# A SwiGLU feed-forward with its down products laid between the block products, on a ring of ten hidden tiles

## Chip, core and metric

The kernel runs on one core of one Trainium2 chip. The metric is the device time of one launch in microseconds (us).

## What is computed

One step of a layer over 520 columns, 512 of a prompt and 8 samples. All of it is in float32.

```python
def half_ffn(x, g, w1, w3, w2):
    h = rmsnorm(x, g)
    return x + 0.5 * ((jax.nn.silu(h @ w1) * (h @ w3)) @ w2)
...
x = half_ffn(x, ...)          # first feed-forward
x = x + mixer(rmsnorm(x))     # short convolution and dilated attention
x = half_ffn(x, ...)          # second feed-forward
y = rmsnorm(x)
```

The width is 1024 (8 blocks of 128) and the hidden width 2816 (22 blocks). The change is in the two feed-forwards.

## The kernel before

**Layout.** The residual lies in SBUF transposed, as eight tiles X[0..7] of 128 features by 520 columns, and every product is done in two halves of 260 columns. A float32 operand is split into a high and a low part of a type that TensorE takes, and `mm3` makes a product from three matmuls: high x high, high x low, low x high. `load_w` brings a block of weights (`raw`, four buffers), ScalarE writes its high part and VectorE its low part (three buffers each).

**A feed-forward (`ffn`)** has four sorts of work.
- Its norm: `rstd_rows` sums squares over the partitions with matmuls (L178, L179) and gives `rbc`, one over the root mean square of each column. The operand of part 0 is X times the gain, split (L135, L136), without the norm; the norm is put on the products after. In the first feed-forward the first three block products are laid ahead of this (`early`), step by step as X arrives.
- Part 0: the hidden blocks 0 to 3, each a plain product of w1 and one of w3 (48 matmuls each), then silu, a multiplication, and the split into `hh` and `hl`. After each block `x_sums(k)` prepares seven sums and differences of normed X blocks, tiles `sh` and `sl` in the pool `xo`.
- The blocks 4 to 21 in nine pairs (`pair(m)`): a pair's two blocks of w1 come out of seven quarter-size products (`seven`, 7 x 12 matmuls) in the way of Strassen and Winograd, and its two blocks of w3 out of another seven. `seven` needs sums of weights (`ws`, L363 to L366, on VectorE), their splits (L372 on ScalarE, L373 on VectorE), and copies and additions of what the products leave in PSUM (L380 to L392). The last additions (L386, L390, L392) stand on VectorE.
- `down(w2, k0, k1)`: the hidden blocks k0 to k1 times w2, added to X. It is eight products, one for each X tile, of 6 matmuls for each hidden block, and each ends in an X update by VectorE (L404), one instruction for each half.

**Order.** `CUTS = (0, 4, 14, 22)`: part 0, then `down` over it; pairs 4 to 12, `down` over these ten blocks; pairs 14 to 20, `down` over the last eight, which in the second feed-forward is interlocked with the final norm (`finish`, `give`). The order within an engine is set before the run by the tile framework, which plans the program in time with the order of the code as priority. Within each engine instructions then run in that order.

**PSUM.** `psum_tile` hands out tiles of two banks: two buffers of the tag "mm" and one of "m3", in the order mm, mm, m3. Tiles of one tag are given out in order.

**SBUF.** Pools stack up from the left and from the right, and a pool may lie on bytes that a closed pool held; its tiles then wait for that one's users. In the feed-forward `gu` (12,480 bytes a partition), `hida` (four hidden blocks, 16,640) and `hidb` (six more, 24,960) lie left from byte 84,640 on; `xo` (58,368), then `xa` (33,280, the operand of part 0) or, later, `su` (the weight sums) lie right. After the first feed-forward the mixer takes `yp` and `ap` left and `xam` right (33,280 bytes, up to byte 229,344), its operand.

Of the kernel before, what the change touches and what calls it, by code (L numbers as in the profile page):

```python
# [13 lines left out]
P = 128  # L14
# [24 lines left out]
CUTS = (0, 4, 14, 22)  # L39
# [12 lines left out]
def tile_step(ctx: ExitStack, tc: tile.TileContext, xT, w0, w1a, w3a, w2a, w_in, w_out, w1b, w3b, w2b,  # L52
# [173 lines left out]
    def ffn(i, w1, w3, w2, g, psum, finish=None):  # L226
        turn = [0]
# [15 lines left out]
        with ExitStack() as st:  # L243
            gu = st.enter_context(tc.tile_pool(name=f"gu{i}", bufs=1, reuse_waits="tile"))
            hids = [st.enter_context(tc.tile_pool(name=f"hida{i}", bufs=1, reuse_waits="tile"))]
            with ExitStack() as sx:
                xo = sx.enter_context(tc.tile_pool(name=f"xo{i}", bufs=1, side="right", reuse_waits="tile"))
                with tc.tile_pool(name=f"xa{i}", bufs=1, side="right", reuse_waits="tile") as xa:
                    early = []

                    def start_x():
                        SP.dma_start(gv, gvec)
                        SP.dma_start(X[0][:, TH:], xT[:, 0, TH:])

                    if i == 0:
                        SP.dma_start(X[0][:, :TH], xT[:, 0, :TH])
                        for k in range(0, KD, 2):
                            if k:
                                SP.dma_start(X[k], xT[:, k])
                            early.append(load_w(w0[k // 2], 6, [slice(0, 3), slice(3, 6)] if not k else None, then=start_x if not k else None))  # L260
                            SP.dma_start(X[k + 1], xT[:, k + 1])
                        SP.dma_start(ident, idm)
                    xh, xl, sums = x_operand(xa, f"f{i}", g, i == 0)

                    def norm_tiles():
                        t = psum_tile()
                        return [t[:, h] for h in range(2)]

                    rstd_rows(norm_tiles, sums, D, rbc)
                    if early:  # L270

                        early, ws = [psum_tile() for _ in range(3)], early
                        for k in range(KD):
                            for e, ps in enumerate(early):
                                hi, lo = (t[:, 3 * (k % 2) + e] for t in ws[k // 2])
                                for h in range(2):
                                    c = slice(h * TH, (h + 1) * TH)
                                    mm3(ps[:, h, :TH], hi, lo, xh[k][:, c], xl[k][:, c], k == 0, k == KD - 1)
                    xs = []
                    for m in range(CUTS[1]):  # L280
                        pp = []
                        a = gu.tile([P, T], F32, name="a", tag="a", bufs=2)
                        b = gu.tile([P, T], F32, name="b", tag="b")
                        for w, t in ((w1, a), (w3, b)):
                            if early:

                                A.activation(halves(t), early.pop(0)[:, :, :TH], AF.Copy)
                                pp.append(halves(t))
                                continue
                            hi, lo = load_w(w[m], KD)  # L290
                            ps = psum_tile()
                            gemm(ps, [(hi, lo, 0, KD)], xh, xl)
                            pp.append(ps[:, :, :TH])
                        V.tensor_tensor(halves(a), pp[0], halves(rbc), ALU.mult)
                        A.activation(a, a, AF.Silu)
                        V.tensor_tensor(halves(b), pp[1], halves(rbc), ALU.mult)
                        V.tensor_tensor(b, b, a, ALU.mult)
                        hh, hl = hidden(m)
                        A.activation(hh, b, AF.Copy)
                        V.tensor_tensor(hl, b, hh.bitcast(F32), ALU.subtract)  # L300

                        xs.append(x_sums(xo, xa, f"f{i}", g, m))
                    down(w2, 0, CUTS[1], Hh, Hl, psum_tile)
                hids.append(st.enter_context(tc.tile_pool(name=f"hidb{i}", bufs=1, reuse_waits="tile")))
                su = sx.enter_context(tc.tile_pool(name=f"su{i}", bufs=2, side="right", reuse_waits="tile"))

                def pair(m):

                    at, aw, bt = psum_tile(), psum_tile(), psum_tile()
                    a = gu.tile([P, 4, TH], F32, name="a", tag="a", bufs=2)  # L310
                    b = gu.tile([P, 4, TH], F32, name="b", tag="b")
                    x = seven(su, w1, m, xs, at, aw[:, 0, :TH], a)
                    A.activation(a[:, 0:2], a[:, 0:2], AF.Silu)
                    A.activation(a[:, 3], a[:, 3], AF.Silu, scale=-1.0)
                    A.activation(a[:, 2], x, AF.Silu, scale=-1.0)
                    x = seven(su, w3, m, xs, bt, aw[:, 1, :TH], b)
                    V.tensor_tensor(b[:, 0:2], b[:, 0:2], a[:, 0:2], ALU.mult)
                    V.tensor_tensor(b[:, 3], b[:, 3], a[:, 3], ALU.mult)
                    V.tensor_tensor(b[:, 2], x, a[:, 2], ALU.mult)
                    for r, sign in ((0, 1.0), (1, -1.0)):  # L320
                        hh, hl = (halves(t) for t in hidden(m + r))
                        of = b[:, 2 * r:2 * r + 2]
                        A.activation(hh, of, AF.Copy, scale=sign)
                        if r:
                            V.scalar_tensor_tensor(hl, of, sign, hh.bitcast(F32), ALU.mult, ALU.subtract)
                        else:
                            V.tensor_tensor(hl, of, hh.bitcast(F32), ALU.subtract)
# [67 lines left out]
    def down(w2, k0, k1, Hh, Hl, psum_tile, finish=None):  # L395
# [18 lines left out]
        if not finish:  # L414
            return
# [522 lines left out]
```

## Time and profile before

| | |
|---|---|
| time, median of 3 runs | 1033.15 us (1032.54 to 1035.03) |
| the profiled execution: its time | 1036.0 us |
| its span (first to last instruction) | 1034.2 us |
| mean granted clock of TensorE | 0.981 |
| busy: TensorE matmul (PE) | 996.0 us, 96% |
| TensorE weight load (PEld, overlaps PE) | 965.4 us, 93% |
| VectorE (DVE) | 726.5 us, 70% |
| ScalarE (ACT) | 505.0 us, 49% |
| GpSimd (POOL) | 92.2 us, 9% |

Busy time is that of the profiled execution. Consecutive matmuls overlap in the records, so a stretch of TensorE can count as busy though matmuls follow each other more slowly than they could. A row of the trace names an engine, the line of the kernel, the operation, and the tiles written and read.

### The profile page before, as it was taken

What the parts mean: (1) busy time and instruction counts of PE and PEld (TensorE: products, weight loads), DVE (VectorE), ACT (ScalarE), POOL (GpSimd) and SP (SyncE); (2) the same over time, 40 slices, a digit from 0 to 9 for tenths busy, and PEclk for the clock granted to TensorE, in tenths of its full rate; (3) what the DMA queues carried; (4) which work ended last, traced back from release to release, by engine and by line L of the source; (5) the groups of instructions that cost most, each with busy time, mean ns of one, the idle gap of its engine ahead of it and who ended that gap; (6) DMA issues with size and microseconds to landing.
All of it is one profiled execution on the core that took longest, in us unless ns stands there. A gap on an engine that the chain in (4) does not pass through costs nothing.

```text
span 1034.2 us, 19174 instructions
## 1 busy us (share of the span) xinstructions
PE 996.0 (96%) x7897; PEld 965.4 (93%) x7897; DVE 726.5 (70%) x1193; ACT 505.0 (49%) x833; POOL 92.2 (9%) x103
## 2 busy tenths in 40 slices
PE   6999999999999999999999998999999999999997
PEld 5999999999999999999999897999998999999897
DVE  6788888436786546667688799797887634788332
ACT  4534565323555436566565545443555422555342
POOL 1000000000000031112022263000000000000022
PEclk6999999999999999999999999999999999999998
DMA  6325434354443445243246665325334233333302
GB/s 208 113 90 186 144 131 140 105 183 156 148 157 125 143 141 173 83 144 129 66 146 222 205 203 184 103 82 184 133 125 151 64 90 113 102 103 103 101 22 83
DMA packets 37912, 136.62 MB, mean 132 GB/s; under 512 B 5760, under 2 KB 8512, under 8 KB 37312
## 3 DMA queue, kind: packets, MB, share of 16 engines
q1 hardware_dynamic: 37824, 135.39, 39.2%
q8 instruction: 62, 1.02, 0.4%
q14 instruction: 26, 0.21, 0.1%
HBM read 131.07 MB, written 37.82 MB: 163 GB/s over the span
## 4 chain that ended last, share of the span: by engine, by line
PE 70%; DVE 15%; DMA 6%; issue 4%; ACT 4%; POOL 1%; SPq 0%; POOLq 0%; DVEq 0%; ACTq 0%
PE ps L121 22%; PE ps L123 21%; PE ps L122 21%; DVE lo L373 3%; DMA raw<-in_w1b 2%; DVE lo L109 2%; DMA raw<-in_w3b 2%; DVE ls L373 1%; ACT hi L108 1%; PE s L568 1%; DMA raw<-in_w1a 1%; DVE ws L364 1%; DVE raw L365 1%; ACT hi L372 1%; DVE ws L363 1%
## 5 line engine op out<-in xcount | busy, mean ns | idle before, releaser
L108 ACT ACTIVATE hi<-raw 128x1024 fp32r<-128x1024 f32 (+3 forms) x136 | 119.1, 878 | 215.6 <-PE ps L122 167.3
L121 PE MATMUL ps<-hh,hi 128*128 128x260 f32 x704 | 200.5, 287 | 4.3 <-ACT hi L108 3.5
L123 PE MATMUL ps<-hh,lo 128*128 128x260 f32 x704 | 200.8, 286 | 1.5 <-DVE lo L109 1.4
L122 PE MATMUL ps<-hl,hi 128*128 128x260 f32 x704 | 199.9, 285 | 0.5 <-DVE hl L300 0.3
L109 DVE TENSOR_TENSOR lo<-raw,hi 128x1024 fp32r<-128x1024 f32 (+3 forms) x136 | 143.6, 1057 | 74.9 <-ACT hi L108 74.0
L121 PEld LDWEIGHTS ps<-hh,hi 128*128 128x128 f32 x704 | 133.5, 191 | 6.8 <-ACT hi L108 4.3
L123 PEld LDWEIGHTS ps<-hh,lo 128*128 128x128 f32 x704 | 134.0, 190 | 3.0 <-DVE lo L109 2.5
L122 PEld LDWEIGHTS ps<-hl,hi 128*128 128x128 f32 x704 | 134.0, 190 | 1.2 <-DVE hl L300 1.2
L121 PE MATMUL ps<-mh,hi 128*128 128x260 f32 x384 | 110.3, 288 | 1.8 <-DVE q L498 1.1
L123 PE MATMUL ps<-mh,lo 128*128 128x260 f32 x384 | 109.3, 285 | 0.3 <-DVE u L619 0.3
L122 PE MATMUL ps<-ml,hi 128*128 128x260 f32 x384 | 109.4, 285 | 0.0
L372 ACT ACTIVATE hi<-raw 128x1024 fp32r<-128x1024 f32 x72 | 75.7, 1053 | 60.8 <-PE ps L122 58.2
L144 POOL TENSOR_TENSOR acc<-acc,sq 128x520 f32<-128x520 f32 (+1 forms) x25 | 38.3, 1530 | 752.9 <-ACT sq L143 748.8
L373 DVE TENSOR_TENSOR lo<-raw,hi 128x1024 fp32r<-128x1024 f32 x72 | 87.5, 1217 | 4.8 <-ACT hi L372 4.8
L372 ACT ACTIVATE hs<-ws 128x1024 fp32r<-128x1024 f32 x72 | 60.5, 840 | 54.0 <-DVE ws L364 48.0
L121 PE MATMUL ps<-f1sh,hi 128*128 128x260 f32 x288 | 82.1, 285 | 3.4 <-DVE X L404 1.2
L121 PE MATMUL ps<-f0sh,hi 128*128 128x260 f32 x288 | 82.2, 286 | 2.0 <-ACT a L384 1.7
L122 PE MATMUL ps<-f0sl,hi 128*128 128x260 f32 x288 | 81.4, 283 | 0.0
L123 PE MATMUL ps<-f1sh,lo 128*128 128x260 f32 x288 | 80.2, 282 | 1.3 <-DVE lo L373 1.2
L122 PE MATMUL ps<-f1sl,hi 128*128 128x260 f32 x288 | 81.3, 283 | 0.0
L123 PE MATMUL ps<-f0sh,lo 128*128 128x260 f32 x288 | 79.6, 282 | 0.0
L404 DVE SCALAR_TENSOR_TENSOR X<-ps,X 128x260 f32<-128x260 f32 x96 | 36.7, 422 | 57.9 <-PE ps L123 57.9
(278 smaller groups left out, 2744.8 us busy)
## 6 DMA issues: line engine op xcount, KB each, us to landing
out_cko<-in_ck SPq DMA_DIRECT2D x16, 1023.0 KB, 7.1
out_cvo<-in_cv SPq DMA_DIRECT2D x16, 1023.0 KB, 7.2
raw<-in_w_in SPq DMA_DIRECT2D x24, 512.0 KB, 3.3
raw<-in_w1b SPq DMA_DIRECT2D x22, 512.0 KB, 3.3
raw<-in_w3b SPq DMA_DIRECT2D x22, 512.0 KB, 3.3
raw<-in_w3a SPq DMA_DIRECT2D x21, 512.0 KB, 3.3
raw<-in_w1a SPq DMA_DIRECT2D x20, 512.0 KB, 3.3
raw<-in_w2a SPq DMA_DIRECT2D x16, 320.0 KB, 3.0
```

The lines of the kernel that those rows point to most:

```text
L108: A.activation(hi, raw, AF.Copy)
L109: V.tensor_tensor(lo, raw, hi.bitcast(F32), ALU.subtract)
L121: PE.matmul(out, lhsT=hi, rhs=xh, start=start, stop=False, skip_group_check=more)
L122: PE.matmul(out, lhsT=hi, rhs=xl, start=False, stop=False, skip_group_check=more)
L123: PE.matmul(out, lhsT=lo, rhs=xh, start=False, stop=stop, skip_group_check=more)
L144: G.tensor_tensor(dst[:, c], dst[:, c], sq[:, c], ALU.add)
L363: V.tensor_tensor(s[:, 0], rb[:, :KQ], rb[:, KQ:], ALU.add)
L364: V.tensor_tensor(s[:, 1], s[:, 0], ra[:, :KQ], ALU.add)
L365: V.tensor_tensor(rb[:, :KQ], rb[:, :KQ], ra[:, :KQ], ALU.add)
L372: A.activation(h, f, AF.Copy)
L373: V.tensor_tensor(l, f, h.bitcast(F32), ALU.subtract)
L404: V.scalar_tensor_tensor(X[m][:, c], ps[:, h, :TH], 0.5, X[m][:, c], ALU.mult, ALU.add)
```

## The change

The middle of each feed-forward is ordered anew.
- `CUTS` has four parts: blocks 0 to 3, 4 to 9, 10 to 13, 14 to 21. The hidden blocks lie on a ring of ten tiles, block m on tile m mod 10.
- `down` of all parts but the last gives back a list of eight products instead of doing them. `FILLS` says how many of the products of the part before are done at each pair: half of them between its two `seven`, the rest behind it. The products of part 0 so lie between pairs 4 to 8, those of blocks 4 to 9 between pairs 10 and 12, those of blocks 10 to 13 between pairs 14 to 18.
- The X update is one instruction of 520 columns.
- A fourth PSUM tile ("m4", pool `ps4`) takes turns with the three, until the last `down` begins. The banks of the final norm (`psN`) are opened only at its end.
- `xo` lies left, between `hida` and `hidb`, and stays to the end of the feed-forward.

```diff
-CUTS = (0, 4, 14, 22)
+CUTS = (0, 4, 10, 14, 22)
+RING = 10
+
+
+FILLS = {4: 3, 6: 3, 8: 2, 10: 4, 12: 4, 14: 3, 16: 3, 18: 2, 20: 0}
...
         def psum_tile():
             turn[0] += 1
-            pool, tag = (psum, "m3") if turn[0] % 3 == 0 else (psM, "mm")
+            pools = [(psM, "mm"), (psM, "mm"), (psum, "m3")] + [(p, "m4") for p in more]
+            pool, tag = pools[turn[0] % len(pools)]
             return pool.tile([P, 2, 512], F32, name="ps", tag=tag)
...
-            at = m - max(c for c in CUTS if c <= m)
+            at = m % RING
...
-            with ExitStack() as sx:
-                xo = sx.enter_context(tc.tile_pool(name=f"xo{i}", bufs=1, side="right", reuse_waits="tile"))
...
+            xo = st.enter_context(tc.tile_pool(name=f"xo{i}", bufs=1, reuse_waits="tile"))
+            more.append(sx.enter_context(tc.tile_pool(name=f"ps4{i}", bufs=1, space=PSUM)))
+            todo = []
+
+            def fill(n):
+
+                for _ in range(min(n, len(todo))):
+                    todo.pop(0)()
...
-                    down(w2, 0, CUTS[1], Hh, Hl, psum_tile)
...
+            todo += down(w2, 0, CUTS[1], Hh, Hl, psum_tile)
+            hids.append(st.enter_context(tc.tile_pool(name=f"hidb{i}", bufs=1, reuse_waits="tile")))
+            su = sx.enter_context(tc.tile_pool(name=f"su{i}", bufs=2, side="right", reuse_waits="tile"))
...
+            def pair(m, n):
...
+                A.activation(a[:, 2], x, AF.Silu, scale=-1.0)
+                fill(n)
+                x = seven(su, w3, m, xs, bt, aw[:, 1, :TH], b)
...
-                for c0, c1 in zip(CUTS[1:], CUTS[2:]):
-                    for m in range(c0, c1, 2):
-                        pair(m)
-                    if c1 < KF:
-                        down(w2, c0, c1, Hh, Hl, psum_tile)
...
+            for c0, c1 in zip(CUTS[1:], CUTS[2:]):
+                for m in range(c0, c1, 2):
+                    n = FILLS[m]
+                    pair(m, n // 2)
+                    fill(n - n // 2)
+                if c1 < KF:
+                    todo += down(w2, c0, c1, Hh, Hl, psum_tile)
             preload()
+            sx.close()
+            more.clear()
             down(w2, CUTS[-2], KF, Hh, Hl, psum_tile, finish)
...
-        for m in range(KD - 2 if finish else KD):
+        def whole(m):
             ws = parts(m)
             ps = psum_tile()
             gemm(ps, ws, Hh, Hl)
-            for h in range(2):
-                update(m, ps, h)
+            V.scalar_tensor_tensor(halves(X[m]), ps[:, :, :TH], 0.5, halves(X[m]), ALU.mult, ALU.add)
             if finish:
                 finish(m, None)
+
+        if k1 < KF:
+            return [lambda m=m: whole(m) for m in range(KD)]
+        for m in range(KD - 2 if finish else KD):
+            whole(m)
...
-    with ExitStack() as st_f, tc.tile_pool(name="psB", bufs=1, space=PSUM, reuse_waits="tile") as psB:
+    with tc.tile_pool(name="psB", bufs=1, space=PSUM, reuse_waits="tile") as psB, ExitStack() as st_f:
...
+                part["ps"] = st_f.enter_context(tc.tile_pool(name="psN", bufs=1, space=PSUM))
...
-            ps = psB.tile([P, 512], F32, name=f"nps{h}", tag=f"n{h}")
+            ps = part["ps"].tile([P, 512], F32, name=f"nps{h}", tag=f"n{h}")
```

## Rows read from the trace of the kernel before

**Rows 1.** The page's first part: busy time, share of span, instructions.

```profile
PE 996.0 (96%) x7897; PEld 965.4 (93%) x7897; DVE 726.5 (70%) x1193; ACT 505.0 (49%) x833; POOL 92.2 (9%) x103
```

**Rows 2.** Busy time by stretch (from:to), first feed-forward.

```profile
core 0: us, PE busy (x) PEld busy (x) DVE busy (x) ACT busy (x) POOL busy (x), PEclk, DMA share, GB/s
...
27.00:66.00 39.00, 39.00 (x329) 39.00 (x328) 34.58 (x52) 21.83 (x25) 0.00 (x0) 1.00 0.31 96
66.00:92.00 26.00, 25.00 (x202) 24.20 (x202) 19.61 (x35) 8.63 (x13) 0.00 (x0) 1.00 0.55 182
92.00:200.00 108.00, 106.00 (x867) 104.26 (x865) 85.81 (x131) 59.16 (x104) 0.00 (x0) 1.00 0.40 136
200.00:255.00 55.00, 54.87 (x453) 54.52 (x454) 25.11 (x41) 14.15 (x20) 0.00 (x0) 1.00 0.50 166
255.00:344.00 89.00, 87.24 (x717) 86.03 (x715) 66.14 (x99) 46.51 (x81) 0.00 (x0) 1.00 0.40 137
344.00:352.00 8.00, 6.72 (x40) 6.17 (x38) 2.26 (x3) 2.87 (x3) 0.00 (x0) 0.79 0.54 199
```

**Rows 3.** Busy time by stretch, second feed-forward.

```profile
694.00:719.00 25.00, 24.69 (x202) 24.02 (x201) 17.83 (x31) 8.28 (x12) 0.00 (x0) 1.00 0.43 148
719.00:831.00 112.00, 106.82 (x868) 104.53 (x867) 86.09 (x133) 59.09 (x103) 0.00 (x0) 1.00 0.36 122
831.00:886.00 55.00, 54.46 (x449) 54.10 (x450) 25.32 (x42) 14.51 (x20) 0.00 (x0) 1.00 0.36 109
886.00:976.00 90.00, 88.00 (x720) 86.52 (x718) 66.69 (x100) 47.20 (x82) 0.00 (x0) 1.00 0.31 100
```

**Rows 4.** Waits of TensorE in 719 to 831 us.

```profile
engine line waited for: us in total, times, longest us
PE ps L121 <- DVE X L404: 1.2, 1, 1.2
PE ps L123 <- DVE lo L373: 1.2, 1, 1.2
```

**Rows 5.** Groups of VectorE by line and shape, 92 to 200 us.

```profile
L373 DVE TENSOR_TENSOR lo<-raw,hi 128x1024 fp32r<-128x1024 f32 x19 | 23.1, 1218 | 1.7 <-ACT hi L372 1.7
L373 DVE TENSOR_TENSOR ls<-ws,hs 128x1024 fp32r<-128x1024 f32 x9 | 10.9, 1215 | 0.0
L364 DVE TENSOR_TENSOR ws<-ws,raw 128x512 f32<-128x512 f32 x9 | 6.2, 686 | 0.1
L373 DVE TENSOR_TENSOR ls<-ws,hs 128x512 fp32r<-128x512 f32 x9 | 6.1, 682 | 0.0
```

**Rows 6.** The start: busy time of 5 to 23 us, the norm's first matmul, its reader.

```profile
5.00:23.00 18.00, 10.09 (x36) 7.50 (x36) 15.36 (x20) 9.73 (x16) 4.10 (x3) 0.62 0.74 258
...
23.35 0.58 PE L178 MATMUL ps<-rhi,ones_r 128*128 128x260 f32 x1 [2.17 <-ACT rhi L171]
...
27.84 0.43 DVE L182 TENSOR_SCALAR rv<-ps 128x260 f32<-128x260 f32 x1 [3.81 <-PE ps L179]
```

**Rows 7.** Timelines at the end of part 0, both feed-forwards.

```profile
64.25 4.01 DVE L351 TENSOR_TENSOR f0sl<-f0z,f0sh 128x1820 fp32r<-128x1820 f32 x2
...
66.65 0.28 PE L123 MATMUL ps<-f0h,lo 128*128 128x260 f32 x1
...
71.53 0.70 DVE L300 TENSOR_TENSOR hl<-b,hh 128x520 fp32r<-128x520 f32 x1 [0.71 <-ACT hh L299]
...
694.68 0.28 PE L123 MATMUL ps<-f1h,lo 128*128 128x260 f32 x1
...
698.74 0.70 DVE L300 TENSOR_TENSOR hl<-b,hh 128x520 fp32r<-128x520 f32 x1 [0.70 <-ACT hh L299]
```

**Rows 8.** Busy time of 348 to 350 us, in the last down products' start.

```profile
348.00:350.00 2.00, 2.00 (x11) 2.00 (x11) 0.00 (x0) 0.00 (x0) 0.00 (x0) 0.50 1.73 700
```

**Rows 9.** Timelines: the mixer operand's first split, a memset, the second feed-forward's splits.

```profile
383.86 0.71 ACT L135 ACTIVATE mh<-X,gv 128x520 fp32r<-128x520 f32 x1
...
389.77 0.06 DVE L619 MEMSET u<- 128x2 f32 x1
...
643.25 5.05 ACT L135 ACTIVATE f1h<-X,gv 128x520 fp32r<-128x520 f32 x8
```

**Rows 10.** The page's costliest groups: the X updates.

```profile
L404 DVE SCALAR_TENSOR_TENSOR X<-ps,X 128x260 f32<-128x260 f32 x96 | 36.7, 422 | 57.9 <-PE ps L123 57.9
```

More of the change, by code (lines that the diff above doesn't have):

```diff
@@ L226, in ffn @@
     def ffn(i, w1, w3, w2, g, psum, finish=None):
-        turn = [0]
+        turn, more = [0], []
         def psum_tile():
             turn[0] += 1
-            pool, tag = (psum, "m3") if turn[0] % 3 == 0 else (psM, "mm")
+            pools = [(psM, "mm"), (psM, "mm"), (psum, "m3")] + [(p, "m4") for p in more]
+            pool, tag = pools[turn[0] % len(pools)]
             return pool.tile([P, 2, 512], F32, name="ps", tag=tag)
@@ L241, in hidden @@
             return Hh[m], Hl[m]
-        with ExitStack() as st:
+        with ExitStack() as st, ExitStack() as sx:
             gu = st.enter_context(tc.tile_pool(name=f"gu{i}", bufs=1, reuse_waits="tile"))
             hids = [st.enter_context(tc.tile_pool(name=f"hida{i}", bufs=1, reuse_waits="tile"))]
-            with ExitStack() as sx:
-                xo = sx.enter_context(tc.tile_pool(name=f"xo{i}", bufs=1, side="right", reuse_waits="tile"))
[L248 to L275, printed above, removed]
-                                for h in range(2):
[L277 to L302, printed above, removed]
-                    down(w2, 0, CUTS[1], Hh, Hl, psum_tile)
[L304 to L327, printed above, removed]
-                for c0, c1 in zip(CUTS[1:], CUTS[2:]):
-                    for m in range(c0, c1, 2):
-                        pair(m)
-                    if c1 < KF:
-                        down(w2, c0, c1, Hh, Hl, psum_tile)
@@ new lines, in ffn @@
+            todo += down(w2, 0, CUTS[1], Hh, Hl, psum_tile)
+            hids.append(st.enter_context(tc.tile_pool(name=f"hidb{i}", bufs=1, reuse_waits="tile")))
+            su = sx.enter_context(tc.tile_pool(name=f"su{i}", bufs=2, side="right", reuse_waits="tile"))
+            def pair(m, n):
+                at, aw, bt = psum_tile(), psum_tile(), psum_tile()
+                a = gu.tile([P, 4, TH], F32, name="a", tag="a", bufs=2)
+                b = gu.tile([P, 4, TH], F32, name="b", tag="b")
+                x = seven(su, w1, m, xs, at, aw[:, 0, :TH], a)
+                A.activation(a[:, 0:2], a[:, 0:2], AF.Silu)
+                A.activation(a[:, 3], a[:, 3], AF.Silu, scale=-1.0)
+                A.activation(a[:, 2], x, AF.Silu, scale=-1.0)
+                fill(n)
+                x = seven(su, w3, m, xs, bt, aw[:, 1, :TH], b)
+                V.tensor_tensor(b[:, 0:2], b[:, 0:2], a[:, 0:2], ALU.mult)
+                V.tensor_tensor(b[:, 3], b[:, 3], a[:, 3], ALU.mult)
+                V.tensor_tensor(b[:, 2], x, a[:, 2], ALU.mult)
+                for r, sign in ((0, 1.0), (1, -1.0)):
+                    hh, hl = (halves(t) for t in hidden(m + r))
+                    of = b[:, 2 * r:2 * r + 2]
+                    A.activation(hh, of, AF.Copy, scale=sign)
+                    if r:
+                        V.scalar_tensor_tensor(hl, of, sign, hh.bitcast(F32), ALU.mult, ALU.subtract)
+                    else:
+                        V.tensor_tensor(hl, of, hh.bitcast(F32), ALU.subtract)
@@ L409, in down @@
             gemm(ps, ws, Hh, Hl)
-            for h in range(2):
-                update(m, ps, h)
+            V.scalar_tensor_tensor(halves(X[m]), ps[:, :, :TH], 0.5, halves(X[m]), ALU.mult, ALU.add)
             if finish:
                 finish(m, None)
+        if k1 < KF:
+            return [lambda m=m: whole(m) for m in range(KD)]
+        for m in range(KD - 2 if finish else KD):
+            whole(m)
         if not finish:
@@ L822, in give @@
             fp, c = part["p"], slice(h * TH, (h + 1) * TH)
-            both = [ps, psB.tile([P, 512], F32, name="nps0", tag="n0")] if h else [ps]
+            both = [ps, part["ps"].tile([P, 512], F32, name="nps0", tag="n0")] if h else [ps]
             for p in both:
```

48 lines of the change are left out of this document (added).

## The prediction

> **What bounds the kernel now.** I read the page first: TensorE is busy 996.0 of the span [rows 1]. That leaves 38 us, so the question is where TensorE waits, not what it does; the change removes no matmul. A matmul lasts 0.28 us in the trace but the next one starts much sooner, so small waits don't show in the busy time. I therefore counted matmuls by stretch. In 27 to 66 us nothing waits: 39.0 us for 329, of which about two only reach in from the edges, is 39.0/327 = 0.1193 us each [rows 2]. Every other stretch is held against that pitch, two matmuls taken off its count:
>
> First feed-forward [rows 2]: the down products of part 0 (66 to 92) lose 26 - 200 x 0.1193 = 2.1; the pairs of part 1 (92 to 200) 108 - 865 x 0.1193 = 4.8; its down products (200 to 255) 1.2; the pairs of part 2 (255 to 344) 3.7. Sum 11.8. Second [rows 3]: 1.1, 8.7, 1.7 and 4.3, sum 15.8. So the whole middle holds 27.6 us that an order of work could win, 2.7% of the time. The chain of waits there names VectorE more than anything: an X update 1.2, a weight's low part 1.2 in the pairs of the second feed-forward [rows 4].
>
> A rule speaks against reading this from matmul time: the Trainium skill, "Perfetto Trace Analysis", Identifying the Most-Contended Engine, says that matmul busy time is no good measure of the room left, and LDWEIGHTS busy time is. By the matmul busy time of the eight stretches the room would be 12.9 us, by LDWEIGHTS 21.8 [rows 2, 3]; the trace agrees with the rule as far as it goes, and the count of matmuls gives still more, 27.6.
>
> The stretches also differ in VectorE: 85.8 us busy of 108 in the pairs, 25.1 of 55 in the down products [rows 2]. In a pair it works 0.79 of the time, so any lateness comes through; in the down products it rests and runs ahead.
>
> **The first gain: down products laid between.** A pair is 2 x 7 x 12 = 168 matmuls, 20.0 us. VectorE has 85.8/5 = 17.2 of work in it. With three down products of 24 between (8.6 us) its load falls from 0.79 to about (17.2 + 3 x 1.5)/28.6 = 0.76 (1.5 us a down product: a conversion at 0.69, as for a tile of that size in [rows 5], and the X update at 2 x 0.42 [rows 10]). The waits for VectorE should go, and those where ScalarE is still occupied with the last pair's hidden tiles too, since a down product now stands there. What stays: each block product's accumulator has to be copied out before the next use. I take a third of what the pair stretches lose: 2.8 of 8.5 and 4.3 of 13.0. Bounds: 0.6 each (the conversion at the last border, which isn't touched) and everything. The 1.2 and 1.7 of the old down stretches go.
>
> **The fourth PSUM buffer.** At the start only one of the first three columns runs while the norm is awaited: 36 matmuls in 5 to 23 us, then the norm's matmul, 2.17 us late [rows 6]. The tile of the norm and that of the first column share a tag and come in order. With four in turn, two columns have tags of their own: 36 more matmuls fit into that wait, 36 x 0.1193 = 4.3 us. But it buys no time by itself: VectorE sets when part 0 is done (next), so TensorE only arrives earlier at a wait. Its share is that the norm, whose result VectorE awaits for 3.81 us [rows 6], comes sooner.
>
> **The first loss: the border after part 0.** Today part 0's products end at 66.65 and VectorE ends part 0 only at 71.53 + 0.70 = 72.2; in between and until 92, TensorE does 192 down products, under which VectorE prepares the first pair [rows 7]. Now the first pair comes next. Its first seven needs the sums x_sums(3) (in the first feed-forward the last f0sl ends at 68.3 [rows 7]), four weight sums at 0.69, a conversion at 1.22 and one at about 1.2 [rows 5]: 5.2 us of VectorE, less 1.4 (12 x 0.1193) that TensorE's first product covers, 3.8. VectorE's end of part 0 moves forward by two conversions of w2 that are not yet due (2 x 0.69) and by what the earlier norm gives (0 to 3.8, taken as 3.1): 72.2 - 4.5 + 3.8 = 71.5, a hole of 71.5 - 66.7 = 4.8 against today's end (the lead above widens it on TensorE's side by as much as it gains). One down product, 24 x 0.1193 = 2.9 us, can fill part of it if its PSUM tile is given out in time; its tag may come behind the pair's third tile. Between 0 and 2.9 I take 1.4. In the second feed-forward there is no early norm: 698.74 + 0.70 - 1.4 + 3.8 = 701.8, against 694.7 on TensorE: 7.1, less 1.4. There 48 more matmuls may be queued ahead of the norm, which I price at 0.7 (0 to 2.6).
>
> After a hole TensorE runs slow: behind the wait at 344 us the granted clock is 0.50, the lower level of 1.2 GHz [rows 8], and 344 to 352 has 38 matmuls in 8.0 us, 3.5 lost, of which TensorE is idle for only 1.28 [rows 2]. So 2.2 for the clock, at each border.
>
> First: 11.8 - 4.8 + 1.4 - 2.2 - 2.8 = +3.4. Second: 15.8 - 7.1 + 1.4 - 2.2 - 4.3 - 0.7 = +2.9.
>
> **The second loss: the pools.** xo (58,368 bytes a partition) moves to the left. gu, hida, xo and hidb now end at 84,640 + 12,480 + 16,640 + 58,368 + 24,960 = 197,088, and the mixer's operand pool xam begins at 229,344 - 33,280 = 196,064 (tile sizes added up). They overlap by 1,024 bytes, which they did not before. Today mh is written during the last down products (at 383.86, and so on for each X [rows 9]). How a pool waits for the one it lies on is seen elsewhere: u's memset, which reads nothing, comes only at 389.77, behind the last down product, though VectorE had idle time; f1h's eight splits came in one block of 5.05 us at 643.25, after the last reader of the pool beneath [rows 9]. The same is now due for mh: eight splits after 388 in place of one. Least cost 0.5 (only the first waits), most 5.1 (the block, on the path); TensorE has three columns to do meanwhile, and the norm moves back: 3.0.
>
> The rest is free. The X update becomes one instruction of 520 columns for two of 260 at 0.42 [rows 10], eight more per feed-forward; TensorE covers them, and if not, the border above pays. The same weights are loaded in as many transfers. psN takes ps4's banks at the end, where ps4 was long released.
>
> **Sum.** 3.4 + 2.9 - 3.0 = 3.3 us. Against the profiled execution, 1036.0 (1.8 of it around the span of 1034.2), that is 1032.7; its median run was 1033.15, so I predict **1029.9**.
>
> **Rivals.**
> All waits go (R1). VectorE's mean load in the interleaved stretch is under TensorE's, and if it never comes late, both remainders fall to 0.6: 2.2 + 3.7 more, 1024; with a whole down product in each hole (1.5 more each) and the pool at its least (2.5 more), 1018.5. For it: the old down products of part 1, with VectorE resting, lose only 1.2 in 55 us [rows 2]. Against: a pair still needs its sums within 20 us. The Trainium skill, same page, Optimization Strategy, has it so: where regimes differ in their contended engine, interleaving them may help; no figure is given.
>
> Slower (R2): VectorE at the border. The second seven needs its own sums: 4 x 0.69 + 2 x 1.22 + 1.22 + 0.68 = 7.1 us [rows 5]. If that doesn't fit under the first seven's 10 us, each border is later by up to 7.1, and both by 14.2: 1044. It decides against the change by more than 0.3% from 3.2 us a border on: 1029.9 + 6.4. For it: VectorE is 0.89 busy in 27 to 66 [rows 2], so nothing can be done ahead. Likely 1040.
>
> No change (R3): the waits in pairs are mostly copies out of PSUM, not want of other work; half stay rather than a third: 3.6 back, 1033.5.
>
> **How the numbers follow.** Forecast 0.33 (1025 to 1035), R1 0.25 (1018.5 to 1026), R2 0.22 (1036 to 1044), R3 0.20 (1031 to 1037). 0.3%, 3.1 us, is about what a measurement can tell. Faster than 1030.05: R1 and over half of the forecast, 0.44; within: 0.31; slower than 1036.25: 0.25. For 8 in 10 the range runs from the middle of R1 to the middle of R2, 1020 to 1040; it takes in the bounds of hole, pool and remainder one at a time.
>
> **What would show it.** In the profile after: two columns (72 matmuls) before the norm at 23 us; a hole in TensorE of some us near 62 to 72 and 695 to 702 with a granted clock of 0.50 behind it; then stretches of pairs with 0.1193 us a matmul almost throughout and VectorE between 0.70 and 0.80; mh in a block at 388. Wrong if TensorE goes on at the border without a hole (faster), if the pairs lose as much as now, or if mh is written as early as today.

## The result: 2.8% slower

The changed kernel takes 1064.44 us (median of 4 runs, 1061.29 to 1065.19) beside 1033.75 us for the kernel before on the same chip: a ratio of 1.0282, 95% interval 1.0241 to 1.0324 (estimated from all runs; the two medians by themselves stand at 1.0297). The forecast was 1029.9, range 1020 to 1040: neither the sign nor the range held. The profiled execution took 1061.29 us with a span of 1059.5, 25.3 more than before. That is less than the 30.7 between the medians, since the profiled execution of before was a long one (1036.0) and that of after the shortest of its four; what follows accounts for the 25.3.

The page's first part, of the changed kernel, answers to [rows 1]:

```profile
PE 999.2 (94%) x7897; PEld 968.2 (91%) x7897; DVE 736.4 (70%) x1163; ACT 510.5 (48%) x833; POOL 89.8 (8%) x103
```

The count of matmuls is the same. TensorE's busy time is up by 3.2 us and the span by 25.3, so nearly all of the change is waiting. Busy time by stretch, columns as in [rows 2]: the border behind part 0, the pairs with the down products between them, then the same for the second feed-forward, and four microseconds inside the first border:

```profile
61.00:95.00 34.00, 26.47 (x195) 25.04 (x193) 26.28 (x35) 15.64 (x26) 0.00 (x0) 0.90 0.30 101
95.00:351.00 256.00, 247.99 (x2027) 244.27 (x2028) 175.93 (x261) 116.72 (x191) 0.00 (x0) 1.00 0.43 145
...
708.00:743.00 35.00, 27.52 (x195) 26.01 (x193) 26.42 (x35) 15.35 (x25) 0.00 (x0) 0.85 0.36 128
743.00:1002.00 259.00, 249.23 (x2026) 246.59 (x2027) 176.38 (x261) 118.20 (x191) 0.00 (x0) 0.99 0.35 111
70.00:74.00 4.00, 3.98 (x19) 3.68 (x19) 3.93 (x6) 1.99 (x4) 0.00 (x0) 0.55 0.61 191
```

Held against the pitch of 0.1193 us, two matmuls taken off as in the prediction, they lose 34 - 193 x 0.1193 = 11.0; 256 - 2025 x 0.1193 = 14.4; 12.0; 17.5. The stretches that were to be freed of waits lose more than before. VectorE is busy for only 0.69 of the second stretch (175.93 of 256), so it isn't short of time there.

Every kernel below was read in the same way, but from counts of matmuls, so that all can be compared: the loss over the first 192 matmuls behind part 0's last (the border), over the next 2,016 (pairs and down products), and the mixer's length (its first product to the first of the second feed-forward). The change of the span, part by part, from the starts of those matmuls in both traces, one execution each; the forecast column gathers the prediction's terms in the same way:

| part | before | after | change | forecast |
|---|---|---|---|---|
| first: end of part 0 | 66.65 | 60.91 | -5.7 | |
| first: border loss | 2.1 | 10.7 | +8.6 | +3.5 with part 0 |
| first: pairs and downs | 9.5 | 14.6 | +5.1 | -6.9 |
| first: last down products | 3.8 | 1.6 | -2.2 | 0 |
| mixer, length | 255.4 | 263.5 | +8.1 | +3.0 |
| second: part 0, length | 50.7 | 50.1 | -0.5 | |
| second: border loss | 1.3 | 11.6 | +10.4 | +7.5 with part 0 |
| second: pairs and downs | 13.8 | 17.8 | +4.0 | -10.4 |
| second: last downs, end | | | -2.3 | 0 |
| sum | | | +25.3 | -3.3 |

Where a pair waits now. What VectorE waited for in 95 to 345 us (engine, line, tile awaited, total us, times, longest):

```profile
DVE ws L380 <- DMA raw<-in_w1a: 19.0, 7, 3.6
DVE lo L390 <- ACT hi L389: 12.1, 12, 4.4
DVE ws L380 <- DMA raw<-in_w3a: 9.1, 5, 2.8
```

In the pairs and downs of before (92 to 345 us), the same two waits of the weight sums for their loads are

```profile
DVE ws L363 <- DMA raw<-in_w1a: 5.2, 6, 1.7
DVE ws L363 <- DMA raw<-in_w3a: 4.4, 6, 1.4
```

Weights of the pairs now come late. One such case, followed in time through the timelines of ScalarE, SyncE's queue, VectorE and TensorE:

```profile
246.77 1.06 ACT L389 ACTIVATE hi<-raw 128x1024 fp32r<-128x1024 f32 x1 [4.15 <-issue]
...
248.29 2.35 DVE L390 TENSOR_TENSOR lo<-raw,hi 128x1024 fp32r<-128x1024 f32 x2
...
249.53 1.47 SPq L117 DMA_DIRECT2D raw<-in_w1a  x2
...
254.74 0.63 ACT L112 ACTIVATE hi<-raw 128x512 fp32r<-128x512 f32 x1 [2.37 <-PE ps L126]
...
254.97 0.69 DVE L380 TENSOR_TENSOR ws<-raw 128x512 f32<-128x512 f32 x1 [3.59 <-DMA raw<-in_w1a]
...
256.42 1.06 ACT L389 ACTIVATE hs<-ws 128x1024 fp32r<-128x1024 f32 x1 [0.78 <-DVE ws L381]
...
257.53 0.39 PE L125 MATMUL ps<-f0sh,hs 128*128 128x260 f32 x1 [1.03 <-ACT hs L389]
```

ScalarE writes a pair's high part only at 246.77, after 4.15 us of standing. The profile names no releaser ("issue"), but TensorE's last read of an earlier high part, a matmul of L126, runs from 246.40 to 246.68, just ahead of it. The low part (248.29) follows; only then is the raw tile free, and SyncE loads the next pair's w1 (249.53); it lands at about 255, after VectorE has stood still for 3.59 us; sums, split, and TensorE stops for 1.03 us.

Last, the mixer's operand: ScalarE's timeline at the end of the first feed-forward, which answers to the first line of [rows 9].

```profile
393.52 4.46 ACT L139 ACTIVATE mh<-X,gv 128x520 fp32r<-128x520 f32 x7 [3.44 <-PE ps L126]
```

Seven splits come in one block behind the last reader of the feed-forward's pools, as the second loss of the prediction had it.

### The profile page after: what moved, and what is told of

Same layout as the page of the kernel before. It is cut to its first block, busy times and chain, and to the rows that moved or that the text cites. A ratio compares the mean times of both kernels' runs of the same rounds, so it can differ in the third digit from the quotient of the medians.

```text
span 1059.5 us, 19111 instructions
## 1 busy us (share of the span) xinstructions
PE 999.2 (94%) x7897; PEld 968.2 (91%) x7897; DVE 736.4 (70%) x1163; ACT 510.5 (48%) x833; POOL 89.8 (8%) x103
## 4 chain that ended last, share of the span: by engine, by line
PE 68%; DVE 14%; DMA 9%; issue 4%; ACT 4%; POOL 1%; SPq 0%; POOLq 0%; DVEq 0%; ACTq 0%
PE ps L125 21%; PE ps L127 21%; PE ps L126 21%; DVE lo L390 3%; DMA raw<-in_w1a 3%; DVE lo L113 2%; DMA raw<-in_w3a 2%; DMA raw<-in_w1b 2%; ACT hs L389 1%; DMA raw<-in_w3b 1%; PE s L589 1%; DVE ws L381 1%; ACT hi L389 1%; ACT hi L112 1%; DVE ws L380 1%
## 5 line engine op out<-in xcount | busy, mean ns | idle before, releaser
L112 ACT ACTIVATE hi<-raw 128x1024 fp32r<-128x1024 f32 (+2 forms) x136 | 118.8, 876 | 182.4 <-PE ps L126 131.6
L126 PE MATMUL ps<-hl,hi 128*128 128x260 f32 x704 | 199.8, 284 | 0.0
L113 DVE TENSOR_TENSOR lo<-raw,hi 128x1024 fp32r<-128x1024 f32 (+2 forms) x136 | 143.8, 1059 | 43.3 <-ACT hi L112 42.2
L126 PEld LDWEIGHTS ps<-hl,hi 128*128 128x128 f32 x704 | 134.0, 190 | 0.0
L126 PE MATMUL ps<-ml,hi 128*128 128x260 f32 x384 | 110.6, 288 | 1.4 <-DVE ml L140 1.4
L390 DVE TENSOR_TENSOR lo<-raw,hi 128x1024 fp32r<-128x1024 f32 x72 | 87.5, 1222 | 25.5 <-ACT hi L389 25.3
L126 PE MATMUL ps<-f1sl,hi 128*128 128x260 f32 x288 | 81.9, 284 | 3.7 <-DVE f1sl L368 3.7
L126 PE MATMUL ps<-f0sl,hi 128*128 128x260 f32 x288 | 81.4, 283 | 4.0 <-DVE f0sl L368 4.0
L427 DVE SCALAR_TENSOR_TENSOR X<-ps,X 128x520 f32<-128x520 f32 x62 | 43.2, 697 | 52.8 <-PE ps L127 52.4
L125 PEld LDWEIGHTS ps<-mh,hi 128*128 128x128 f32 x384 | 73.4, 191 | 4.5 <-issue 3.9
```

Of the source, the lines that this page charges most:

```text
L112: A.activation(hi, raw, AF.Copy)
L113: V.tensor_tensor(lo, raw, hi.bitcast(F32), ALU.subtract)
L125: PE.matmul(out, lhsT=hi, rhs=xh, start=start, stop=False, skip_group_check=more)
L126: PE.matmul(out, lhsT=hi, rhs=xl, start=False, stop=False, skip_group_check=more)
L390: V.tensor_tensor(l, f, h.bitcast(F32), ALU.subtract)
L427: V.scalar_tensor_tensor(halves(X[m]), ps[:, :, :TH], 0.5, halves(X[m]), ALU.mult, ALU.add)
```

## Experiments

Sixteen further kernels. Times are medians; the ratio is against the kernel before on the same chip, with its 95% interval, estimated from all runs as above; losses as defined above, first / second feed-forward. The losses are of one profiled execution each, and executions of one kernel differ by some us (before, on all chips: 1029.9 to 1037.6). e4 and e5 leave out the loads of w2 for the interleaved products, and e9 to e12 the low part of the sums in the matmuls, so these six compute something else.

| run | us | ratio | border | pairs and downs | mixer |
|---|---|---|---|---|---|
| before | 1033.75 | | 2.1 / 1.3 | 9.5 / 13.8 | 255.4 |
| after | 1064.44 | 1.0282 | 10.7 / 11.6 | 14.6 / 17.8 | 263.5 |
| e1 xo right | 1049.20 | 1.0160 (1.0142 to 1.0179) | 10.9 / 7.3 | 15.4 / 14.9 | 255.4 |
| e2 down0 block | 1040.89 | 1.0079 (1.0053 to 1.0105) | 6.7 / 1.2 | 12.2 / 13.0 | 263.3 |
| e3 before, four PSUM | 1029.17 | 0.9958 (0.9941 to 0.9976) | 6.6 / 1.2 | 12.0 / 8.2 | 255.4 |
| e4 no weights in fills | 1021.49 | 0.9889 (0.9867 to 0.9911) | 5.3 / 6.0 | 2.8 / 1.6 | 262.8 |
| e5 convert only | 1022.22 | 0.9899 (0.9871 to 0.9926) | 7.3 / 6.8 | 2.3 / 1.6 | 262.8 |
| e6 own raw | 1059.65 | 1.0245 (1.0213 to 1.0277) | 11.1 / 8.0 | 21.2 / 20.6 | 257.0 |
| e7 right, block | 1035.75 | 1.0031 (1.0009 to 1.0052) | 6.5 / 1.2 | 13.8 / 12.9 | 255.5 |
| e8 block, own raw | 1080.64 | 1.0454 (1.0433 to 1.0475) | 17.6 / 17.3 | 22.0 / 24.3 | 256.9 |
| e9 no low sums | 1047.92 | 1.0175 (1.0119 to 1.0230) | 12.2 / 7.1 | 16.5 / 11.6 | 255.5 |
| e10 own raw, two | 1048.08 | 1.0155 (1.0123 to 1.0187) | 11.3 / 8.9 | 13.5 / 13.2 | 258.4 |
| e11 own high, low | 1022.00 | 0.9896 (0.9869 to 0.9923) | 8.0 / 6.1 | 1.8 / 2.2 | 255.6 |
| e12 own all | 1024.55 | 0.9922 (0.9896 to 0.9947) | 10.1 / 9.7 | 3.1 / 3.1 | 255.4 |
| e13 ring of eight | 1017.19 | 0.9845 (0.9816 to 0.9874) | 8.4 / 6.3 | 2.2 / 1.2 | 255.4 |
| e14 its block | 1019.46 | 0.9854 (0.9827 to 0.9880) | 9.0 / 7.1 | 2.0 / 1.2 | 258.2 |
| e15 e13, own placed | 1016.01 | 0.9828 (0.9802 to 0.9854) | 6.2 / 5.5 | 1.5 / 1.0 | 258.3 |
| e16 e14, own placed | 1014.40 | 0.9812 (0.9782 to 0.9842) | 6.4 / 4.6 | 3.4 / 1.2 | 255.5 |

### One part of the change undone, or done alone (e1 to e4)

**e1**, against the changed kernel:

```diff
-            xo = st.enter_context(tc.tile_pool(name=f"xo{i}", bufs=1, reuse_waits="tile"))
+            xo = sx.enter_context(tc.tile_pool(name=f"xo{i}", bufs=1, side="right", reuse_waits="tile"))
```

> The changed kernel with xo back on the right side; all else as changed, so hidb no longer ends above the first byte of the mixer's operand pool. Theory (the pools delay the mixer's operand): the mixer, 260.4 us from its first product to the last before the second feed-forward, goes back to the 252.3 us of before, and the time from 1064.4 to about 1056. Rival (the mixer starts late because VectorE and ScalarE come out of the last down products with more undone work): the mixer stays within 2 us of 260 and the time between 1062 and 1066.

The mixer goes back to 255.4 us, the length of before, and the operand's splits stand one by one again behind their X updates, as two lines of ScalarE's timeline in e1 show:

```profile
383.73 0.72 ACT L139 ACTIVATE mh<-X,gv 128x520 fp32r<-128x520 f32 x1
...
389.47 0.72 ACT L139 ACTIVATE mh<-X,gv 128x520 fp32r<-128x520 f32 x1
```

So the pool theory holds, with 8.1 us. The kernel gained 15.2, more than either expectation: the second border and the second pairs gave 4.3 and 3 too. In the second, the last sums of X (f1sl) begin 3.7 us behind part 0's last matmul in the changed kernel and 0.9 in e1, and TensorE waits 3.7 us for them beside 1.6; what held them up with xo on the left was not followed.

**e2** (the changed kernel with `FILLS` 0 for pairs 4, 6 and 8, and `fill(KD)` ahead of the first pair):

> The changed kernel with all eight down products of part 0 done ahead of the first pair, as before; the other two parts stay interleaved. Theory (the border costs because VectorE has to prepare the first pair with nothing under it): of the first 192 matmuls after part 0 the loss goes from 11.0 and 12.0 us to about 2 each, part 0's lead of 5.7 us comes through or is partly lost in a wait for VectorE; time 1044 to 1050. Rival (VectorE has too much work from there on, so the wait only moves into the pairs): at most 8 us come back, 1056 or more.

23.5 us came back, more than forecast. The borders fall to 6.7 and 1.2, and the pairs, which now have no down products between them up to pair 10, lose less as well (12.2 and 13.0).

**e3**, on the kernel before:

```diff
+                more.append(sx.enter_context(tc.tile_pool(name=f"ps4{i}", bufs=1, space=PSUM)))
...
-            pool, tag = (psum, "m3") if turn[0] % 3 == 0 else (psM, "mm")
+            pools = [(psM, "mm"), (psM, "mm"), (psum, "m3")] + [(p, "m4") for p in more]
+            pool, tag = pools[turn[0] % len(pools)]
```

> The kernel before with the fourth PSUM tile alone (and the final norm's banks opened late, which it needs). Theory of the prediction (two columns run under the wait for the norm, but VectorE sets the end of part 0, so it buys nothing): 1031 to 1037. Rival (the earlier norm brings VectorE forward too, and the 5.7 us by which part 0 ends earlier in the changed kernel come through): 1027 to 1030.

Between the two: 0.4% faster. In the first feed-forward part 0 ends 6.3 us earlier (60.33), and the border takes 4.5 of that back and the pairs 2.5; TensorE waits at 66 us for the last hidden tile, as the prediction said (its timeline in e3):

```profile
66.25 0.71 PE L121 MATMUL ps<-hh,hi 128*128 128x260 f32 x3 [2.41 <-ACT hh L301]
68.16 0.59 PE L122 MATMUL ps<-hl,hi 128*128 128x260 f32 x1 [1.20 <-DVE hl L302]
```

Most of the gain is in the second feed-forward, whose pairs lose 8.2 in place of 13.8. The Trainium skill, "Perfetto Trace Analysis", Matmul Optimizations, asks that all eight PSUM banks be in use; this run agrees, by 0.4%.

**e4** (`down` of the interleaved parts takes tiles of `xo` as weights):

```diff
         def parts(m):
+            if of:
+                return [(of[0][0][:, :, :P], of[0][1][:, :, :P], k, n) for k in range(k0, k1, n)]
```

> The changed kernel in which the interleaved down products take resident tiles as weights: their matmuls and X updates stay, but the loads of w2, its conversions by ScalarE and VectorE and its turns in the raw, high and low buffers are left out (the last part's stay), so the output is another. Theory (the weights of the down products take the buffers from the pairs' weights, which are then loaded and converted late): the loss behind the first 192 matmuls, 14.3 and 17.5 us, falls under 8 in sum, and the time to 1036 to 1044. Rival (the pairs wait for copies out of PSUM and for X updates, whatever the weights do): above 1054.

The pairs lose 2.8 and 1.6, and the kernel is at 1021.49, more of a gain than forecast. It isn't the matmuls between, their PSUM tiles or the X updates that cost: it is their weights.

### Conversions, raw buffers, or high and low buffers (e5 to e12)

**e5** (e4, with the conversions done into a scratch tile):

```diff
             if of:
+                j = wp.tile([P, 3, P], F32R, name="jk", tag="jk", bufs=1)
+                cs = (slice(0, n // 2), slice(n // 2, n))
+                for c in cs:
+                    A.activation(j[:, :n // 2], of[0][0][:, c, :P].bitcast(F32), AF.Copy)
+                    V.tensor_tensor(j[:, :n // 2], of[0][0][:, c, :P].bitcast(F32), j[:, :n // 2].bitcast(F32), ALU.subtract)
...
```

> As the run whose interleaved products take resident tiles as weights (1021.5 us), but ScalarE and VectorE convert as many weights for them as in the changed kernel, from a resident tile into a scratch tile that nothing waits for; the loads of w2 and the turns in the raw, high and low buffers stay left out, and the output is another. Theory (the buffers' turns make the pairs' weights late, not the time that conversions take): at most 1031. Rival (ScalarE and VectorE are short of time for the conversions of w2): 1045 or more. In between, both share.

1022.22 against 1021.49: the time of the conversions costs nothing that can be measured. What is left is the loads and the turns in the buffers.

**e6** (e1, with one small raw buffer for the interleaved products):

```diff
...
+        for c in (slice(0, n // 2), slice(n // 2, n)):
+            r = wp.tile([P, 3, P], F32, name="rawd", tag="rawd", bufs=1)[:, :n // 2]
+            if c.start:
+                SP.dma_start(r, src[:, c])
+            else:
+                load(r, src[:, c])
+            A.activation(hi[:, c], r, AF.Copy)
+            V.tensor_tensor(lo[:, c], r, hi[:, c].bitcast(F32), ALU.subtract)
```

> The changed kernel with xo on the right (1049.2 us), in which the interleaved products load their w2 blocks in two halves through a small raw buffer of their own (1,536 bytes), so that the four raw buffers serve the pairs alone; high and low parts still take turns in the same three buffers each. Theory (the turn of the raw buffers is what makes the pairs' weights late; VectorE stands idle for loads of w1 for 19.0 us in the pairs of the first feed-forward): half or more of the 15.0 and 14.9 us lost behind the first 192 matmuls comes back, 1032 to 1038. Rival (three high and three low buffers are the narrow place, the raw ones follow them): 1045 to 1051.

Both theories fall: 10 us slower than e1. The single buffer is waited for in two places, by SyncE's queue (the next half can't be loaded) and by ScalarE (the half isn't there yet), in 95 to 345 us:

```profile
SPq L130 <- DMA rawd<-in_w2a: 36.1, 15, 4.7
SPq L122 <- DMA rawd<-in_w2a: 28.7, 14, 4.9
...
ACT hi L125 <- DMA rawd<-in_w2a: 41.2, 26, 3.6
```

Whatever of the pairs comes next on either queue stands behind such a wait. SyncE stands no longer in all than in e1 (about 221 us beside 224, its waits in that stretch added up), while ScalarE's 41.2 us are new; which of the two costs the 10 us was not separated. The run tells nothing of the pairs' own buffers.

**e7** (e1 and e2 together) and **e8** (e7 with the edit of e6), planned before that was known:

> The changed kernel with both xo on the right and part 0's down products in a block; the two other parts stay interleaved, with four PSUM tiles. Theory (the two faults are separate, and add up but for the 4.7 us of the second border that both give back): 1064.4 - 15.2 - 23.5 + 4.7 = 1030.4, so 1028 to 1033. Rival (what is left of the interleaving still costs as against the order of before with four PSUM tiles, 1029.2): 1033 to 1038.

> The former with the small raw buffer for the interleaved products of the other two parts. Theory (raw turns): 5 to 10 us less than it, 1021 to 1027. Rival (high and low buffers): no difference beyond 2 us.

e7 comes out 5 us above the sum. It is 6.6 us slower than e3, and differs from it mainly in the interleaving of the two later parts; its pairs lose 26.7 in sum where those of e3 lose 20.2. So what interleaving was left was still a loss. e8 fails as e6 does, and more, 45 us above e7; in its block eight products with such loads come in a row.

Two buffers each of whole size need room. **e9** makes it in e1: every `sl` tile has one tag and `x_sums` returns `h, h`. **e10** to **e12** open a pool `dw` of two buffers and give the interleaved products their own `raw`, their own `hi` and `lo`, or all three. The lines of e11 (e10 takes `raw` from `dw` and the other two from `wp`, e12 all three from `dw`), as far as the tiles go:

```diff
+    def load_own(src, n):
+        q = [P, n, P]
+        raw = wp.tile(q, F32, name="raw", tag="raw", bufs=4)
+        hi = dw[0].tile(q, F32R, name="hid", tag="hid")
+        lo = dw[0].tile(q, F32R, name="lod", tag="lod")
```

> A base for the next three: the changed kernel with xo on the right (1049.2 us), whose matmuls take the high part of the sums of X where they took the low part; the low part is still computed, into one tile that nobody reads, so the output is another and 21,840 bytes a partition come free. No theory speaks of this: as much work on each engine, so 1042 to 1050, less what TensorE waited for the low sums at the two borders, and 12 to 16 us lost behind the first 192 matmuls in each feed-forward.

> The base, in which the interleaved products have two raw buffers of their own, for whole blocks; high and low parts still take turns with the pairs' in the three buffers each. Theory A (the turns of the raw buffers make the pairs' weights late): at least 10 us less than the base. Theory B (the turns of the high and low buffers do): at most 4 us less.

> The base, in which the interleaved products have two high and two low buffers of their own, and share the raw ones. Theory A (raw): at most 4 us less than the base. Theory B (high and low: a conversion stands in ScalarE's order until a matmul has let its buffer go, and holds the raw buffer that long): at least 10 us less.

> The base with both: two raw, two high and two low buffers for the interleaved products. Theories A and B: the loss behind the first 192 matmuls falls to about that of the run without weights for these products (2.8 and 1.6 us; at most 5 each), 18 to 25 us less than the base. Rival (not the buffers but SP's order of loads and the transfers themselves): less than 10 us come back.

Theory B holds: own raw buffers don't change the time (1048.08 against 1047.92; the pairs lose 1.4 us less in sum, the mixer takes 3.0 more), own high and low ones give 25.9 us and bring the pairs to the losses of e4 (1.8 and 2.2). Raw buffers on top are no gain (1024.55). Busy time by stretch in e10 and in e11:

```profile
96.00:341.00 245.00, 235.82 (x1944) 233.14 (x1943) 166.90 (x248) 112.41 (x184) 0.00 (x0) 1.00 0.41 138
```

```profile
95.00:336.00 241.00, 240.78 (x2008) 240.26 (x2007) 168.97 (x254) 112.73 (x187) 0.00 (x0) 1.00 0.43 145
```

The losses are 245 - 1942 x 0.1193 = 13.3 and 241 - 2006 x 0.1193 = 1.7, at about the same VectorE work. In e11 the profile shows no wait of TensorE at all in this stretch. VectorE still waits for loads there (11.6 us for w1): such a wait by itself is no loss here. Whether two more buffers in the common rings, shared by both, would do as much was not tried.

### A kernel that computes everything (e13 to e16)

**e13** finds the room in a smaller ring:

```diff
-CUTS = (0, 4, 10, 14, 22)
-RING = 10
+CUTS = (0, 4, 8, 12, 16, 22)
+RING = 8
...
-FILLS = {4: 3, 6: 3, 8: 2, 10: 4, 12: 4, 14: 3, 16: 3, 18: 2, 20: 0}
+FILLS = {4: 4, 6: 4, 8: 4, 10: 4, 12: 4, 14: 4, 16: 4, 18: 4, 20: 0}
```

with xo right and `load_own` as in e11. **e14** has `FILLS` 0 for pairs 4 and 6 and `fill(KD)` ahead of them.

> A kernel that computes the reference and has own high and low buffers for the interleaved products: xo on the right, parts of 4, 4, 4, 4 and 6 hidden blocks on a ring of eight tiles, which frees 8,320 bytes a partition, enough for two high and two low buffers of 2,048 bytes; four products at each pair but the last; raw buffers shared as before. Theory (the turns of the high and low buffers were the price of interleaving): near the run with such buffers and no low sums, 1022.0, with eight more loads and X updates in each feed-forward, 1020 to 1028, faster than before and than before with four PSUM tiles (1029.2). Rival (the smaller parts load and convert more, and the raw buffers become the narrow place): 1032 or more.

> The former with part 0's down products in a block ahead of the first pair. Theory (the border is a fault of its own: 11.2 and 7.3 us lost over the first 192 matmuls with the pair first, 6.5 and 1.2 with the block): 4 to 10 us less than the former. Rival (with buffers of its own the first down product fills the border): no difference beyond 2 us, or slower, since the later pairs have fewer products between them.

e13 is 1.55% faster than before, better than the 1020 to 1028 expected, and its pairs run almost without loss (stretches behind the borders; 243 - 2019 x 0.1193 = 2.1 and 242 - 2019 x 0.1193 = 1.1):

```profile
95.00:338.00 243.00, 242.41 (x2021) 241.99 (x2020) 173.81 (x262) 112.04 (x190) 0.00 (x0) 1.00 0.44 151
...
720.00:962.00 242.00, 242.00 (x2021) 242.00 (x2020) 175.22 (x263) 112.89 (x191) 0.00 (x0) 1.00 0.32 103
```

e14, with the block, came out 2.3 us slower than e13, where its theory had 4 to 10 less. It told nothing of the border, since the own buffers lay on bytes of part 0's operand pool. Its first conversion of w2 comes only behind the last reader of that pool (ScalarE's timeline in e14):

```profile
67.31 1.15 ACT L123 ACTIVATE hid<-raw 128x512 fp32r<-128x512 f32 x2 [3.29 <-DVE f0sl L381]
```

**e15** and **e16** are e13 and e14 with both high buffers and one low buffer placed left from the start, the other low one right (against e13):

```diff
+            dw[:] = [st.enter_context(tc.tile_pool(name=f"dw{i}", bufs=1, reuse_waits="tile"))]
             xo = sx.enter_context(tc.tile_pool(name=f"xo{i}", bufs=1, side="right", reuse_waits="tile"))
...
-            dw[:] = [sx.enter_context(tc.tile_pool(name=f"dw{i}", bufs=2, side="right", reuse_waits="tile"))]
+            dw.append(sx.enter_context(tc.tile_pool(name=f"dx{i}", bufs=1, side="right", reuse_waits="tile")))
```

> The kernel with a ring of eight and own high and low buffers (1017.2 us), in which both high buffers and one of the two low ones lie left from the start of each feed-forward, no longer on bytes of part 0's operand pool. Theory (the first w2 conversions waited for that pool: in the run with the block the first one starts at 67.3 us, right behind the last of the sums of X): the first down product can now fill the border, which loses 8.4 and 6.3 us, down to 5 to 7 and 4 to 6; 1013 to 1017. Rival (the border is set by VectorE's sums and conversions for the first pair alone): no difference beyond 2 us.

> The same for the kernel with part 0's down products in a block (1019.5 us). Theory: the first conversions of w2 come before part 0 ends, and the first 192 matmuls lose about what they lost with the block and shared buffers, 6.6 and 1.2 us, in place of 9.0 and 7.1; 1009 to 1014, and then faster than with the pair first by 2 or more. Rival (the block waits for something else too): no difference beyond 2 us.

Pair first 1016.01, block first 1014.40: their intervals overlap widely. e15 is within the ranges of its theory, but its 1.2 us against e13 are also within the 2 us of its rival. The borders lose 6.2 and 5.5 in the one, 6.4 and 4.6 in the other. e16's second border did not fall to 1.2, so its expectation failed in part. What stays at the first border is the end of part 0 on VectorE and ScalarE. In e15 TensorE waits there 1.5 us for the sums (f0sl) and 1.3 for the last hidden tile (hh); in e16 for the last hidden tile (its timeline):

```profile
66.94 0.58 PE L138 MATMUL ps<-hl,hid 128*128 128x260 f32 x1 [3.49 <-DVE hl L325]
```

e16 has the lowest median of all, 1.9% under the kernel before, but is not clear of e15.

In e10, e14 and e15 the mixer takes 258.2 to 258.4 us though xo lies right. The 3 us come late in it, behind its 1,400th matmul, and not at the operand; what causes them was not followed.

## Why the prediction was wrong, step by step

**The first gain: down products laid between.** This is the step that failed: -6.9 and -10.4 us forecast, +5.1 and +4.0 measured. It read the waits of the pairs as VectorE's load (its load was to fall from 0.79 to about 0.76, and "the waits for VectorE should go"). The load did fall, to 0.69 of a stretch that the waits themselves lengthen (0.72 in e13, which hardly waits), and the waits grew. The argument counted what each engine has to do and not what it holds while it does it. A `seven` takes two of three high and two of three low buffers; a down product between takes one more of each, until its last matmul. So the next conversion waits for TensorE, the raw tile is not given back, and the load behind it starts late. In before ScalarE stands for high buffers too, 67.8 us from 92 to 344 us (the first two lines below), but 30.2 of it in the old down products of 200 to 255 us (the third). In the changed kernel all 66.4 us of it (the last two, 95 to 351 us) stand among the pairs:

```profile
ACT hi L108 <- PE ps L122: 35.3, 15, 4.7
ACT hi L372 <- PE ps L122: 32.5, 17, 2.4
...
ACT hi L108 <- PE ps L122: 30.2, 12, 4.7
...
ACT hi L389 <- PE ps L126: 37.2, 19, 3.8
ACT hi L112 <- PE ps L126: 29.2, 15, 4.3
```

The total of these waits doesn't tell the loss, though: e13 has 56.4 us of them in 95 to 330 us, with pairs that lose 2.2:

```profile
ACT hi L401 <- PE ps L137: 29.0, 20, 3.8
ACT hid L123 <- PE ps L137: 27.4, 17, 3.9
```

It is the experiments that show the cause. e5 rules out the conversions' time, e10 the raw buffers, and e11 shows the high and low ones: 25.9 us. Which of the two, high or low, is the narrower was not tried, nor whether they must be apart or only more.

**"The rest is free. ... The same weights are loaded in as many transfers."** True of the count. But the same weights are now loaded while the pairs hold the buffers, and that was priced at nothing without naming the cover.

**The rivals.** R1, with all waits gone, had the mechanism of what e11 and e13 reach, but the changed kernel lacked the buffers. R2 put the loss at the border and at VectorE, and its price, 1040 likely, was too small since the pairs lost as well. None of the rivals was a buffer that both streams need, and none reached 1064.

**The first border**, with part 0's lead: +3.5 forecast, +2.9 measured. Most of its pieces were right: two columns before the norm (72 matmuls by 21.1 us), a hole, the lower clock behind it (0.55 granted in 70 to 74 us). The lead was 5.7 us against 4.3, the added border loss 8.6 against 7.8, and the two errors partly cancel. The down product did not come to fill the hole, though: the first stands at 74.60 us.

**The second border**: +7.5 forecast, +9.8 measured. Part of it belongs to xo's place (11.6 falls to 7.3 in e1). The border is no fault of pair first as such: with buffers of its own, pair first and block first lose about as much (e15, e16).

**The second loss: the pools.** The mechanism was right, mh in a block, and the size off: 3.0 forecast within 0.5 to 5.1, 8.1 measured. The bound took the block's length as the most; but the norm of the mixer and the first rotated tiles stand behind the block, too, and TensorE then waits 2.6 us for v and 2.9 us for q, by its waits in 394 to 426 us, where in before it waits 1.1 us for q and not for v. It also left out the clock, which the borders had: over the mixer's first 31.5 us the granted clock is 1.00 in before (first row) and 0.89 in the changed kernel, and all of the 8.1 us are lost within its first 200 matmuls.

```profile
388.50:420.00 31.50, 29.73 (x248) 29.35 (x247) 21.87 (x33) 17.89 (x26) 5.78 (x5) 1.00 0.50 166
...
394.20:425.70 31.50, 24.59 (x179) 23.66 (x179) 21.69 (x29) 18.45 (x29) 2.63 (x4) 0.89 0.38 132
```

**The fourth PSUM buffer**: "it buys no time by itself" holds in the first feed-forward as far as the border goes, and fails in the second: 0.4% in e3.

**The sum.** 28.6 us lie between forecast and measured change of the span: 12.0 and 14.4 from the pairs, 5.1 from the pools, 2.3 from the second border, less 0.6 at the first and 4.5 at the last downs and the end, of which no term spoke (in the first feed-forward the wait at 344 us [rows 2] is gone there; the second was not followed); rounding is the rest.

The section of the Trainium skill that the prediction cites for interleaving ("Perfetto Trace Analysis", Optimization Strategy) also says that a gap that repeats on the engine to be saturated can mean too few buffers for the next tile. The runs agree: with two high and two low buffers more, the pairs of e9 go from losses of 16.5 and 11.6 us to 1.8 and 2.2 (e11), while two raw buffers more leave 13.5 and 13.2 (e10).

## What to carry to other kernels

When work is laid between other work, count the buffers that each holds and for how long before counting busy time: two streams that take turns in one ring of buffers can wait for each other's matmuls, even where every engine has time to spare. Here it helped to give the second stream its own buffers (e11, e13). Look at what bytes these lie on, since a pool on bytes of a closed one brings that one's last reader with it (e14). Too small a buffer of one's own is worse than a shared one: a single raw buffer made the kernel 10 us slower (e6).

## What the runs showed of the hardware that was not expected

Nothing of the chip itself. Of the queues: in e6 SyncE's queue stood for 36.1 and 28.7 us in 250, and ScalarE for 41.2, for loads into one small buffer, in a kernel 10 us slower than e1, although the pairs' loads of 512 KB landed in a median of 3.3 to 3.4 us, beside 3.3 in before (the page's DMA issues).
